# A gated delta rule inside a decoder kernel: its instructions emitted by one clock, in one order for all engines

## The chip, the cores and the metric

One NeuronCore of a Trainium2 chip runs the whole program. The metric is device microseconds (us) for one launch. The engines are named as in the profile: PE (matrix products and transposes; its weight loads are PEld), DVE (vector), ACT (activations, and one of the queues that issue DMAs), POOL (GpSimd) and SP (DMA issue only).

## What is computed

The program is a decoder of several blocks over 512 tokens of width 1024, in fp32. The change lies in one stage, the first half of `parallel_mixers`, after the first feed-forward block:

```python
proj = h @ w_in
qkv, z, a, bt, glu, gates = jnp.split(proj, offs, axis=-1)
qkv = jax.nn.silu(causal_depthwise_conv(qkv, gdn_conv_qkv))      # 4 taps
g = -jnp.exp(gdn_a_log) * jax.nn.softplus(a + gdn_dt_bias)
o = chunk_gated_delta_rule(q, k, v, g, jax.nn.sigmoid(bt))       # 8 heads of 128
o = rms_norm(o, gdn_norm_g) * jax.nn.silu(z)
c = c_lin * jax.nn.sigmoid(c_gate)                               # from glu
c = causal_depthwise_conv(c, conv_dw_w) + conv_dw_b              # 31 taps, 1024 channels
...
S_t = exp(g_t) S_{t-1} (I - beta_t k_t k_t^T) + beta_t k_t v_t^T ; o_t = S_t^T q_t
```

Each head is done in four chunks of 128 tokens. Within a chunk a triangular system is solved (a matrix Y, built from 16 by 16 blocks that are joined to 32, 64 and 128), and the state S passes from chunk to chunk.

## The kernel before

**Products.** A projection unit is one 128-column piece of `w_in`: `wload` (L326 to L332) brings 512 KB into `wr` (two buffers) by one DMA, ACT rounds it to `wh` (L323), and POOL makes the rest `wl` (L324, `now["lo"] = G` in this stage; DVE does it elsewhere). `wh` and `wl` have four buffers each. PE then makes 24 products of 128 by 512 (`mm3`, L212 to L214). The stage has 3 such units per head for q, k and v (`gdn_rows`), one for z (`gdn_z`), two per group of 128 channels of the long convolution (`glu_conv`), and eight gate units (`gate_proj`).

**Rows.** The end of a `gdn_rows` unit takes four taps (one on ACT, three on DVE, L818), Silu on ACT, four transposes on PE, and for k and q the inverse norm: squares on ACT (L770), a power on POOL.

**Decay and blocks.** `gdn_decay` makes exp of the cumulated gate (a broadcast by DMA from `gcrow`, an add on POOL, four exponentials on ACT, L843) and the matrices `mt` and `at`. `mt` goes to DRAM (`sm`). `gdn_blocks`, for a pair of heads, loads the 16 by 16 blocks (`ub`), inverts all 64 in 15 columns of two small DVE operations (L875, L877), writes them (`sy`, `sx`) and loads them back as Y and X.

**Heads.** `gdn_head` first joins the blocks to Y in eight steps, each of a few small products or transposes and one eviction (L918 to L938), then does 4 chunks of 3 dependent steps (PE, then ACT or DVE, then PE again), then the output: squares, small DVE operations, a power and a product on POOL (L982), four transposes (L218) and one DVE operation (L991).

**The long convolution.** 30 taps per group of 128 channels on DVE (L640, 240 in all), accumulating in one PSUM bank (`cv`).

**The order.** Two heads run as a chain, and `phase` interleaves it with filler (the projection units) by a credit of `pe_ns` per step. Work that follows a projection is put off by `after(8000.0, ...)`. `in_order(True)` ties PE to the order of emission. The order of the other engines is set by the scheduler's priorities: the long convolution stands 300 priorities later (`CONV_LATER`, L636), the block columns 100 (`BLOCKS_LATER`, L870). The weight DMAs are issued from ACT (`now["dq"] = A`), the small DMAs of the delta rule from SP.

After the stage come the other gate units, `split_o`, `gated(..., "w_gdn_out")` and `conv_norm`, whose transposes (L653) read all eight groups of the long convolution.

Of the kernel before, what the change touches and what calls it, by code (L numbers as in the profile page):

```python
# [26 lines left out]
CONV_LATER = 300  # L27
BLOCKS_LATER = 100
# [82 lines left out]
def kernel(ctx: ExitStack, tc: tile.TileContext, a: dict, out: bass.AP, upto=99):  # L111
    nc = tc.nc
    V, A, G, PE, S = nc.vector, nc.scalar, nc.gpsimd, nc.tensor, nc.sync
    n_names = [0]
# [77 lines left out]
    pe_ns = [0.0]  # L192
    order = {"on": False, "last": None}

    def placed(inst):

        if order["on"]:
            if order["last"] is not None:
                tc.add_manual_dep(inst.ins, order["last"].name, mybir.DependencyInfo(
                    mybir.DependencyClass.NoSync, mybir.DependencyReason.DATA), reason="order of emission")  # L200
            order["last"] = inst.ins

    def in_order(on):
        order.update(on=on, last=None)

    def mm(o, lhsT, rhs, start=True, stop=True):
        pe_ns[0] += 230.0
        placed(PE.matmul(o, lhsT, rhs, start=start, stop=stop))  # L208

    def mm3(o, lh, rh, start, stop):  # L210
        pe_ns[0] += 680.0
        placed(PE.matmul(o, lh[1], rh[0], start=start, stop=False))  # L212
        placed(PE.matmul(o, lh[0], rh[1], start=False, stop=False))  # L213
        placed(PE.matmul(o, lh[0], rh[0], start=False, stop=stop))  # L214

    def turn(o, x, i):
        pe_ns[0] += 110.0
        placed(PE.transpose(o, x, i))  # L218
# [25 lines left out]
    later = []  # L244

    def after(ns, work_):
        later.append((pe_ns[0] + ns, work_))

    def due(all_=False):

        for i, (t, work_) in enumerate(later):
            if all_ or t <= pe_ns[0]:
                del later[i]
                work_()
                return True
        return False

    def phase(chain, filler, share):

        filler, credit = iter(filler), 0.0  # L260

        def fill():
            before = pe_ns[0]
            if not due() and next(filler, None) is None:
                return None
            return pe_ns[0] - before + 20.0

        for _ in chain:
            credit += share
            while credit > 0:  # L270
                took = fill()
                if took is None:
                    break
                credit -= took
        while fill() is not None:
            pass
# [337 lines left out]
    def glu_conv(c0, c1):  # L614
        w = dram_w("w_in")
        act = acts["b1_1"]
        for c in range(c0, c1):
            if c % 2 == 0:
                cv.setdefault("out", []).append(slot(FT, tag="ma"))
            ps = []  # L620
            for base in (4112, 4112 + 1024):
                p = bank()
                h, l = wload(w, 0, 8, base + c * 128, 128)
                for k in range(8):
                    mm3(p, (h[:, k], l[:, k]), (act.hi(k), act.lo(k)), k == 0, k == 7)
                    if k % 2:
                        yield 1
                ps.append(p)
            pad = work("pad", (128, T + 30))
            V.memset(pad[:, :30], 0.0)  # L630
            A.copy(pad[:, 30:], ps[0])
            sg = work("xr", (128, T))
            A.activation(sg, ps[1], AF.Sigmoid)
            G.tensor_tensor(pad[:, 30:], pad[:, 30:], sg, OP.mult)
            o = cv["out"][c // 2][:, c % 2]
            with tc.high_priority(-CONV_LATER):  # L636
                s_ = bank(tag="cv")
                A.activation(s_, pad[:, 0:T], AF.Identity, bias=cols["convb"][:, c:c + 1], scale=tap31(0, c))  # L638
                for j in range(1, 31):
                    V.scalar_tensor_tensor(s_ if j < 30 else o, pad[:, j:j + T], tap31(j, c), s_, OP.mult, OP.add)  # L640
            yield 1
# [105 lines left out]
    def gdn_rows(h):  # L747
# [4 lines left out]
        kq = slot(FT, (128, 4, 2, 128), "ma")  # L752
        vk = slot(FT, (128, 2, 4, 128), "vk")
        v, kdec = vk[:, 0], vk[:, 1]
        left = [3]

        def ready():
            left[0] -= 1
            if not left[0]:
                gd["rows", h] = kq, v, kdec  # L760
# [11 lines left out]
        def of_v(x):  # L772
            A.copy(v, four_turned(x))
            ready()

        def of_q(x):
            r = tiny((128, 4))
            squares(r, four_turned(x))
            rq = gd["rq"][:, :, h]
            V.tensor_scalar(rq, r, 128.0, 128.0 * RMS_EPS, OP.mult, OP.add)  # L780
            G.tensor_tensor(rq, rq, nhalf[:, :4], OP.pow)
            ready()

        def of_k(x):
            p = four_turned(x)
            s_ = work("sq", (128, 4, 128))
            A.copy(s_, p)
            r = tiny((128, 4))
            squares(r, s_)
            inv_sqrt(r, r, 1.0, RMS_EPS, 4)  # L790
            G.tensor_tensor(s_, s_, r[:, :, None].to_broadcast([128, 4, 128]), OP.mult)

            def back():
                A.copy(kq[:, :, 0], four_turned(s_))
                G.tensor_tensor(kdec, s_, four(gd["kd"], h), OP.mult)
                ready()

            after(8000.0, back)

        for i, then in ((1, of_k), (0, of_q), (2, of_v)):  # L800
            if ("pre", h) in gd:
                p = gd["pre", h][i]
            else:
                hw, lw = wload(w, 0, 8, i * 1024 + h * 128, 128)
                p = bank()
                for k in range(8):
                    mm3(p, (hw[:, k], lw[:, k]), (act.hi(k), act.lo(k)), k == 0, k == 7)
                    if k % 2:
                        yield 1
# [15 lines left out]
            after(8000.0, lambda then=then, xf=xf: then(xf))  # L825
            yield 1
# [7 lines left out]
    def gdn_decay(h):  # L834
        while ("rows", h) not in gd:
            yield 1
        kq, v, kdec = gd["rows", h]
        dt_ = t2((128, 4, 128))
        src = gd["rows"][0:1, 0:1]
        S.dma_start(dt_, bass.AP(tensor=src.tensor, offset=src.offset + h * 128, ap=[[0, 128], [1024, 4], [1, 128]]))  # L840
        G.tensor_tensor(dt_, dt_, gneg[:, None, :].to_broadcast([128, 4, 128]), OP.add)
        for c in range(4):
            A.activation(dt_[:, c], dt_[:, c], AF.Exp, bias=gd["ngc"][:, c, h:h + 1], scale=1.0)  # L843
        yield 1
        yield 1
        mt, at = work("mt", (128, 4, 128)), work("at", (128, 4, 128))
        for cc in range(2):
# [9 lines left out]
            yield 1  # L857
        S.dma_start(chunks(gd["sm"], h % 2), mt)
        gd["decay", h] = [mt, at]
        yield 1  # L860

    def gdn_blocks(h):
# [6 lines left out]
        S.dma_start(ub, blocks(gd["sm"]))  # L869
        with tc.high_priority(-BLOCKS_LATER):  # L870
            V.memset(yb, 0.0)
# [1195 lines left out]
```

## Time and profile before

| | us |
|---|---|
| three runs | 2838.24 (median), 2834.88 to 2845.14 |
| profiled execution | 2842.67 |
| its span, first to last instruction | 2840.9 |
| PE busy | 2678.6 (94% of the span) |
| DVE, ACT, POOL busy | 1368.0, 1062.1, 473.1 |

The profiled execution lies 4.4 us over the median of the runs. Times are counted from the start of the span. A PE record's length is modelled and overlaps the next one, so for the pace of PE the distance from start to start is what to read. "Idle before" a row is what its engine waited, and behind the arrow stands what ended that wait. "issue" is a wait that the profile can't put down to anything.

### The profile page before, as it was taken

The page shows a single profiled execution, that of the slowest core. Times are in us where ns is not written, and L with a number is a line of the kernel's source. Part 1 is how long each engine was busy: PE and PEld are TensorE (multiplying, and loading weights), DVE is VectorE, ACT ScalarE, POOL GpSimd, SP SyncE. Part 2 cuts the span into 40 slices and gives each one's busy share as a digit, 9 for nine tenths or more (in the row PEclk, how much of TensorE's full clock was granted, in tenths as well). Part 3 has the DMA queues.
Part 4 walks back from the last instruction along what each step waited for, and adds up shares of the span by engine and source line. Part 5 has one row for each costly group of instructions (what it writes and reads, how often), then busy time and mean ns, then how long its engine had stood idle before and what let it go on. Part 6 is the DMA issues. An engine that isn't in the chain of part 4 may idle for free.

```text
span 2840.9 us, 34780 instructions
## 1 busy us (share of the span) xinstructions
PE 2678.6 (94%) x13600; PEld 2180.7 (77%) x13600; DVE 1368.0 (48%) x2476; ACT 1062.1 (37%) x1993; POOL 473.1 (17%) x341
## 2 busy tenths in 40 slices
PE   9999986788788999999999999999999999999998
PEld 7888875676666887988888876786687777888887
DVE  3232355665675356445222255476454464632324
ACT  4222235354333342342222244454255464232231
POOL 0101034333332012002100121031002000211010
PEclk9999998899899999999999999999999999999999
DMA  5223353554542523434323233322235122432332
GB/s 190 97 97 96 97 113 61 87 73 72 69 78 45 111 90 126 141 126 156 97 97 97 97 104 113 98 75 79 76 103 100 51 64 89 142 125 97 97 97 82
DMA packets 326324, 277.30 MB, mean 98 GB/s; under 512 B 50360, under 2 KB 278416, under 8 KB 326160
## 3 DMA queue, kind: packets, MB, share of 16 engines
q1 hardware_dynamic: 267072, 232.61, 27.8%
q10 hardware_dynamic: 59088, 42.47, 9.0%
q8 instruction: 107, 1.75, 0.3%
q14 instruction: 57, 0.47, 0.1%
HBM read 256.64 MB, written 20.49 MB: 98 GB/s over the span
## 4 chain that ended last, share of the span: by engine, by line
PE 46%; DVE 4%; POOL 1%; issue 1%; DMA 1%; ACT 1%; DVEq 0%; ACTq 0%; POOLq 0%; SPq 0%
PE mm L212 13%; PE mm L213 13%; PE mm L214 13%; PE mm L208 6%; DMA wr<-in_w_in 1%; DVE m L359 1%; DVE wl L324 1%; PE mm L1690 0%; POOL hr L348 0%; POOL t L1050 0%; ACT wh L323 0%; DVE m L358 0%; PE mm L1448 0%; PE mm L1740 0%; DVE mf L359 0%
## 5 line engine op out<-in xcount | busy, mean ns | idle before, releaser
L324 DVE TENSOR_TENSOR wl<-wr,wh 128x1024 fp32r<-128x1024 f32 (+1 forms) x351 | 427.4, 1218 | 826.5 <-ACT wh L323 825.2
L212 PE MATMUL mm<-x,wl 128*128 128x512 f32 (+3 forms) x2072 | 806.8, 389 | 2.7 <-DVE gsmall L703 2.5
L213 PE MATMUL mm<-x,wh 128*128 128x512 f32 (+3 forms) x2072 | 794.3, 383 | 0.0
L214 PE MATMUL mm<-x,wh 128*128 128x512 f32 (+3 forms) x2072 | 792.2, 382 | 0.0
L323 ACT CAST wh<-wr 128x1024 fp32r<-128x1024 f32 (+2 forms) x425 | 436.4, 1028 | 787.0 <-PE mm L214 529.1
L212 PEld LDWEIGHTS mm<-x,wl 128*128 128x128 f32 (+2 forms) x2072 | 395.9, 191 | 77.5 <-issue 6.6
L214 PEld LDWEIGHTS mm<-x,wh 128*128 128x128 f32 (+2 forms) x2072 | 395.2, 191 | 75.7 <-issue 1.4
L213 PEld LDWEIGHTS mm<-x,wh 128*128 128x128 f32 (+2 forms) x2072 | 396.3, 191 | 70.5 <-issue 1.2
L324 POOL TENSOR_TENSOR wl<-wr,wh 128x1024 fp32r<-128x1024 f32 x74 | 176.7, 2390 | 485.4 <-ACT wh L323 436.8
L324 POOL TENSOR_TENSOR h<-t,h 128x512 fp32r<-128x512 f32 x66 | 101.7, 1542 | 835.8 <-ACT h L323 835.8
L214 PE MATMUL mm<-wh,h 128*128 128x512 f32 x528 | 205.6, 389 | 0.0
L212 PE MATMUL mm<-wh,h 128*128 128x512 f32 x528 | 205.5, 389 | 0.0
L213 PE MATMUL mm<-wl,h 128*128 128x512 f32 x528 | 205.5, 389 | 0.0
L640 DVE SCALAR_TENSOR_TENSOR mm<-pad,cols,mm 128x512 f32<-128x512 f32 x232 | 174.5, 752 | 40.9 <-ACT mm L638 36.2
L214 PEld LDWEIGHTS mm<-wh,h 128*128 128x128 f32 x528 | 99.1, 188 | 20.6
L213 PEld LDWEIGHTS mm<-wl,h 128*128 128x128 f32 x528 | 99.1, 188 | 20.5
L212 PEld LDWEIGHTS mm<-wh,h 128*128 128x128 f32 x528 | 99.1, 188 | 20.4
L543 ACT ACTIVATE t<-mm 128x512 f32<-128x512 f32 x66 | 39.5, 599 | 127.8 <-PE mm L214 127.8
L544 DVE SCALAR_TENSOR_TENSOR t<-t,mm 128x512 f32<-128x512 f32 x66 | 45.4, 688 | 77.4 <-POOL h L324 54.9
L212 PE MATMUL mm<-m,wl 128*128 128x512 f32 (+1 forms) x224 | 81.7, 365 | 0.1
L214 PE MATMUL mm<-m,wh 128*128 128x512 f32 (+1 forms) x224 | 81.1, 362 | 0.0
L213 PE MATMUL mm<-m,wh 128*128 128x512 f32 (+1 forms) x224 | 80.9, 361 | 0.0
(454 smaller groups left out, 3684.8 us busy)
## 6 DMA issues: line engine op xcount, KB each, us to landing
wr<-in_w_in SPq DMA_DIRECT2D x69, 512.0 KB
wr<-in_w_in ACTq DMA_DIRECT2D x53, 512.0 KB
wr<-in_ffn_wg SPq DMA_DIRECT2D x44, 512.0 KB
wr<-in_ffn_wu SPq DMA_DIRECT2D x44, 512.0 KB
wr<-in_ffn_wd SPq DMA_DIRECT2D x44, 512.0 KB
wr<-in_w_ffn_in SPq DMA_DIRECT2D x44, 512.0 KB
wr<-in_w_ffn_out SPq DMA_DIRECT2D x22, 512.0 KB
xd<-m ACTq DMA_DIRECT2D x32, 256.0 KB
```

What stands on the lines that cost most here:

```text
L208: placed(PE.matmul(o, lhsT, rhs, start=start, stop=stop))
L212: placed(PE.matmul(o, lh[1], rh[0], start=start, stop=False))
L213: placed(PE.matmul(o, lh[0], rh[1], start=False, stop=False))
L214: placed(PE.matmul(o, lh[0], rh[0], start=False, stop=stop))
L323: A.copy(hi, src)
L324: (eng or V).tensor_sub(lo, src, hi.bitcast(FT))
L359: V.scalar_tensor_tensor(yh, yh, r, bh, OP.mult, OP.add)
L543: A.activation(sg, ps[0][f], AF.Silu)
L544: V.scalar_tensor_tensor(sg, sg, scale, ps[1][f], OP.mult, OP.mult)
L640: V.scalar_tensor_tensor(s_ if j < 30 else o, pad[:, j:j + T], tap31(j, c), s_, OP.mult, OP.add)
```

## The change

All emission in the stage goes through one loop. Every chain is a generator that yields nanoseconds of PE work (`yield 1300.0`), put in a list by `spawn`. The clock is `pe_ns`, which each product or transpose advances. `step` runs the chain that is due first, or else the next piece of a projection unit. `unit` may have a condition (`may`), and up to three units' weights are loaded ahead. Each engine but SP is then tied to the order of emission (`keep_order`). A second clock, `dve_ns`, adds 180 ns and 1.1 ns per element for each DVE instruction. `fill_dve` emits one item of background work, a block column or a tap of the long convolution, only where `dve_ns` is behind `pe_ns`. What is left of the taps when all else has been emitted is emitted then, and is not tied. The joins of a pair (`gdn_join`) are split off from `gdn_head`, and `gdn_pair` starts the decay of the next pair before them. The weight DMAs move to SP, the small DMAs to ACT. Two memsets move from DVE to POOL. The gate units move into the loop, as units that open when heads are done. The convolution's input is kept in its output tile and copied to `pad` when its taps begin. The products, and the taps, are the same in number.

```diff
+    def keep_order(start):
+        for inst in nc.cur_bb.bb.instructions[start:]:
+            if inst.engine == mybir.EngineType.SP:
+                continue
+            if inst.engine in last:
+                tc.add_manual_dep(inst, last[inst.engine].name, mybir.DependencyInfo(
                     mybir.DependencyClass.NoSync, mybir.DependencyReason.DATA), reason="order of emission")
...
+            if inst.engine == mybir.EngineType.DVE:
+                n = math.prod(k for _, k in inst.outs[0].ap[1:])
+                dve_ns[0] = max(dve_ns[0], pe_ns[0]) + 180.0 + 1.1 * n
...
+    def fill_dve():
+        while dve_ns[0] < pe_ns[0]:
+            todo = background[0] or background[1]
+            if not todo:
+                break
+            start = len(nc.cur_bb.bb.instructions)
+            todo.pop(0)()
+            keep_order(start)
...
-        S.dma_start(blocks(gd["sy"]), yb)
+        background[0].extend([lambda k=k: column(k) for k in range(15, 0, -1)])
+        yield from until(lambda: not background[0])
+        yield 1000.0
+        A.dma_start(blocks(gd["sy"]), yb)
         A.copy(ub, yb.rearrange("p a b -> p b a"))
-        S.dma_start(blocks(gd["sx"]), ub)
+        yield 1000.0
+        A.dma_start(blocks(gd["sx"]), ub)
+        yield 3500.0
         for t, s_ in (("Y", "sy"), ("X", "sx")):
             for i in range(2):
                 m = work(t, (128, 4, 128))
-                S.dma_start(m, chunks(gd[s_], i))
+                A.dma_start(m, chunks(gd[s_], i))
                 gd["decay", h + i].append(m)
-        yield 1
...
+        yield 4000.0
+    def gdn_pair(h):
+        spawn(gdn_decay(h))
+        spawn(gdn_decay(h + 1), 700.0)
+        yield from until(lambda: ("decay", h) in gd and ("decay", h + 1) in gd)
         yield from gdn_blocks(h)
...
+        if h < 6:
+            spawn(gdn_pair(h + 2))
+        spawn(gdn_join(h))
+        spawn(gdn_join(h + 1), 700.0)
...
-            run(gdn_start(), gdn_gates(), gdn_rows(0))
-            while due(True):
-                pass
+            run(gdn_start(), gdn_gates())
             banks(pj=3, tp=1, gt=3, cv=1)
...
+            while True:
+                fill_dve()
+                start = len(nc.cur_bb.bb.instructions)
+                if not step():
+                    break
+                keep_order(start)
+            for left in background[1]:
+                left()
```

**First place: PE at the gates.** Before, behind the last product of the gate projection (`mm_2795`) and the four transposes of its result (L694) stand the products of the first units; between them and L208, which needs the softplus that DVE makes of those transposes, stand 44 rows, 43 of them such products.

```order
L214 MATMUL mm_2795<-x_2456,wh_2790 16x512
L694 MATMUL mm_2822<-ident,xr_2820 128x16 x4
L212 MATMUL mm_2943<-x_2444,wl_2946 128x512
L213 MATMUL mm_2943<-x_2445,wh_2945 128x512
L214 MATMUL mm_2943<-x_2444,wh_2945 128x512
```

Now, on the same engine (L734 is L694 before; `gsmall` holds the gates):

```order
L214 MATMUL mm_2795<-x_2456,wh_2790 16x512
L734 MATMUL mm_2822<-ident,xr_2820 128x16 x4
L208 MATMUL mm_2858<-gsmall_2827,xr_2606 128x32 x2
L765 MATMUL mm_2862<-ident,gsmall_2827 32x128
L212 MATMUL mm_2911<-x_2444,wl_2895 128x512
L213 MATMUL mm_2911<-x_2445,wh_2894 128x512
```

L208 and L765 moved to stand directly behind the transposes, and the first unit behind them.

**Second place: DVE at the outputs of a pair of heads.** Before, for heads 4 and 5 (L991 reads the transposed output; `mm_5935` is the accumulator of one group of the long convolution):

```order
L925 TENSOR_TENSOR X_5907<-mm_6219,sqc_2607 128x512
L640 SCALAR_TENSOR_TENSOR mm_5935<-pad_5929,cols_300,mm_5935 128x512 x12
L640 SCALAR_TENSOR_TENSOR ma_5745<-pad_5929,cols_300,mm_5935 128x512
L991 SCALAR_TENSOR_TENSOR ma_6181<-mm_6176,cols_286,t_6018 128x512
L991 SCALAR_TENSOR_TENSOR ma_6181<-mm_6198,cols_286,t_6083 128x512
L925 TENSOR_TENSOR X_5909<-mm_6225,sqc_2607 128x512
```

Now, for heads 0 and 1 (L1052 is L991 before, L654 is L640; L902 and L904 are the next pair's decay):

```order
L654 SCALAR_TENSOR_TENSOR mm_4569<-pad_4566,cols_293,mm_4569 128x512
L843 TENSOR_SCALAR gsmall_2827<-tiny_4665 128x4
L654 SCALAR_TENSOR_TENSOR mm_4569<-pad_4566,cols_293,mm_4569 128x512 x3
L1052 SCALAR_TENSOR_TENSOR ma_4705<-mm_4724,cols_286,ma_4705 128x512
L654 SCALAR_TENSOR_TENSOR mm_4569<-pad_4566,cols_293,mm_4569 128x512 x4
L1052 SCALAR_TENSOR_TENSOR ma_4705<-mm_4772,cols_286,ma_4705 128x512
L902 SCALAR_TENSOR_TENSOR mt_4778<-mm_4780,gsmall_2827,t_4313 128x128 x2
```

Thirteen taps in one run ahead of an output became runs of three and four.

**Third place: DVE and PE at the end of the stage.** Before, DVE has no tap left behind the last outputs; L324 is the splitting of the heads' outputs (`m`) and of the next weights (`wl`):

```order
L991 SCALAR_TENSOR_TENSOR ma_6685<-mm_6680,cols_286,t_6502 128x512
L991 SCALAR_TENSOR_TENSOR ma_6685<-mm_6702,cols_286,t_6567 128x512
L324 TENSOR_TENSOR m_7121<-ma_4647,m_7120 128x512 x2
L324 TENSOR_TENSOR m_7127<-ma_5500,m_7126 128x512 x2
L324 TENSOR_TENSOR m_7133<-ma_6181,m_7132 128x512
L324 TENSOR_TENSOR wl_6864<-wr_6862,wh_6863 128x1024
```

Now, on DVE:

```order
L1052 SCALAR_TENSOR_TENSOR ma_6545<-mm_6618,cols_286,ma_6545 128x512
L654 SCALAR_TENSOR_TENSOR mm_6416<-pad_6413,cols_300,mm_6416 128x512
L1052 SCALAR_TENSOR_TENSOR ma_6545<-mm_6631,cols_286,ma_6545 128x512
L654 SCALAR_TENSOR_TENSOR mm_6416<-pad_6413,cols_300,mm_6416 128x512 x13
L347 TENSOR_TENSOR wl_6864<-wr_6862,wh_6863 128x1024
```

Behind the last L1052 now stand 75 taps (15 of group 5, and all 30 of groups 6 and 7), with the eight weight splits of the following projection (L347, which is L324 before) between them. On PE before, `conv_norm`'s transposes (L653; `ma_5745` holds groups 6 and 7) come behind the first product unit of `w_gdn_out` (`mm_7144`):

```order
L213 MATMUL mm_7144<-m_7139,wh_7146 128x512
L214 MATMUL mm_7144<-m_7138,wh_7146 128x512
L653 MATMUL mm_7178<-ident,ma_2942 128x128 x2
L653 MATMUL mm_7178<-ident,ma_3688 128x128 x2
L653 MATMUL mm_7185<-ident,ma_5206 128x128 x2
L653 MATMUL mm_7185<-ident,ma_5745 128x128 x2
```

Now, on PE (L693 is L653 before; `ma_5888` holds groups 6 and 7):

```order
L214 MATMUL mm_6990<-x_2456,wh_7023 128x512
L693 MATMUL mm_7178<-ident,ma_3023 128x128 x2
L693 MATMUL mm_7178<-ident,ma_3983 128x128 x2
L693 MATMUL mm_7185<-ident,ma_4959 128x128 x2
L693 MATMUL mm_7185<-ident,ma_5888 128x128 x2
L693 MATMUL mm_7200<-ident,ma_3023 128x128
L212 MATMUL mm_6991<-x_2444,wl_6994 128x512
```

They moved ahead of the last three of that projection's eight units (`mm_6991` is one of them) and of the first unit of `w_gdn_out`.

## Rows read from the trace of the kernel before

**Rows 1.** The page: busy time of PE; granted clock in 40 slices of the span.
```profile
PE 2678.6 (94%) x13600; PEld 2180.7 (77%) x13600; DVE 1368.0 (48%) x2476; ACT 1062.1 (37%) x1993; POOL 473.1 (17%) x341
...
PEclk9999998899899999999999999999999999999999
```

**Rows 2.** Windows: stretch, its length, busy PE, PEld, DVE, ACT, POOL; clock, DMA.
```profile
424.00:992.00 568.00, 463.33 (x2516) 381.47 (x2517) 335.62 (x645) 241.31 (x571) 181.66 (x112) 0.90 0.49 75
```

**Rows 3.** Waits of PE from 424 to 992 us: total, times, longest.
```profile
PE mm L218 <- POOL t L982: 23.8, 8, 8.7
PE mm L218 <- ACT ma L821: 20.3, 1, 20.3
PE mm L208 <- issue: 19.3, 2, 11.6
PE mm L208 <- DVE t L948: 9.9, 3, 3.8
PE mm L218 <- ACT t L770: 8.0, 2, 5.8
PE mm L208 <- DMA X<-sx: 7.7, 1, 7.7
PE mm L208 <- DVE at L856: 6.0, 2, 5.3
```

**Rows 4.** Timeline of PE, products spaced at high and at low clock.
```profile
570.40 0.39 PE L213 MATMUL mm<-x,wh 128*128 128x512 f32 x1
570.63 0.39 PE L214 MATMUL mm<-x,wh 128*128 128x512 f32 x1
...
868.48 0.63 PE L213 MATMUL mm<-x,wh 128*128 128x512 f32 x1
868.91 0.63 PE L214 MATMUL mm<-x,wh 128*128 128x512 f32 x1
```

**Rows 5.** Timeline of PE around the gates.
```profile
408.13 0.60 PE L694 MATMUL mm<-ident,xr 16*128 16x16 f32 x4 [2.39 <-ACT xr L691]
...
411.19 0.76 PE L212 MATMUL mm<-x,wl 128*128 128x512 f32 x1 [2.46 <-DVE gsmall L703]
...
424.16 0.63 PE L208 MATMUL mm<-gsmall,xr 128*128 128x32 f32 x4 [0.79 <-DVE gsmall L719]
```

**Rows 6.** Timeline of PE at the outputs of heads 2 and 3.
```profile
747.82 0.60 PE L208 MATMUL mm<-t,at 128*128 128x128 f32 x4
...
757.67 1.12 PE L218 MATMUL mm<-ident,t 128*128 128x128 f32 x4 [7.87 <-POOL t L982]
...
760.10 1.11 PE L218 MATMUL mm<-ident,t 128*128 128x128 f32 x4 [1.31 <-POOL t L982]
```

**Rows 7.** Timeline at the outputs of heads 4 and 5: DVE and PE.
```profile
855.21 9.46 DVE L640 SCALAR_TENSOR_TENSOR mm<-pad,cols,mm 128x512 f32<-128x512 f32 x12
...
866.21 2.05 PE L208 MATMUL mm<-X,mt 128*128 128x128 f32 x8 [11.65 <-issue]
```

**Rows 8.** Groups on DVE from 424 to 992 us: busy, mean ns, idle before.
```profile
L324 DVE TENSOR_TENSOR wl<-wr,wh 128x1024 fp32r<-128x1024 f32 x12 | 14.7, 1224 | 41.2 <-ACT wh L323 41.2
```

**Rows 9.** Timeline of the first pair's blocks: SP and PE.
```profile
541.34 0.60 SPq L878 DMA_DIRECT2D sy<-yb  x1
...
547.80 2.92 SPq L884 DMA_DIRECT2D X<-sx  x2
...
556.57 3.78 PE L208 MATMUL mm<-X,mt 128*128 128x128 f32 x16 [7.68 <-DMA X<-sx]
```

**Rows 10.** Groups on ACT from 424 to 992 us.
```profile
L956 ACT ACTIVATE t<-mm,gsmall 128x128 f32<-128x128 f32 x32 | 10.3, 366 | 11.6 <-POOL wl L324 9.8 <-PE mm L208 1.6
L843 ACT ACTIVATE t<-t,gsmall 128x128 f32<-128x128 f32 x32 | 10.2, 391 | 19.9 <-POOL t L841 19.9
```

**Rows 11.** Timeline of ACT: a table load and its neighbours.
```profile
742.04 0.81 ACT L949 ACTIVATE t<-mm,gsmall 128x128 f32<-128x128 f32 x2 [3.24 <-DVE t L948]
742.87 1.28 ACT L1005 ACT_TABLE_LOAD   x1
744.17 0.60 ACT L1005 ACTIVATE t<-mm 128x512 f32<-128x512 f32 x1
```

More of the change, by code (lines that the diff above doesn't have):

```diff
@@ L241, in interleave @@
             yield
[L244 to L255, printed above, removed]
-        return False
[L258 to L275, printed above, removed]
-            pass
+    procs, units, loaded, behind, background = [], [], [], [], [[], []]
@@ new lines, in spawn, with split_ahead @@
+    def spawn(g, ns=0.0):
+        procs.append([pe_ns[0] + ns, g])
+    def split_ahead(n):
+        for u in ([u for u in units if u["may"]()] + units)[:n]:
+            if u["w"] is None and sum(e["w"] is not None for e in units) < 3:
+                u["w"] = wload(*u["src"])
+    def fill_dve():
[6 more added lines that the diff above has]
+            keep_order(start)
@@ new lines, in step @@
+    def step():
+        due = [p for p in procs if p[0] <= pe_ns[0]]
+        if due:
+            p = min(due, key=lambda e: e[0])
+            ns = next(p[1], None)
+            if ns is None:
+                procs.remove(p)
+            else:
+                p[0] = pe_ns[0] + ns
+            return True
+        if not behind:
+            u = next((u for u in units if u["may"]()), None)
+            if u is not None:
+                units.remove(u)
+                if u["w"] is None:
+                    u["w"] = wload(*u["src"])
+                behind.append(u["body"](*u["w"]))
+                split_ahead(2)
+        if behind:
+            if next(behind[0], None) is None:
+                behind.pop()
+            return True
+        if procs:
+            pe_ns[0] = min(p[0] for p in procs)
+            return True
+        return False
@@ L279, with unit, until @@
+    def unit(src, body, may=lambda: True):
+        units.append({"src": src, "body": body, "may": may, "w": None})
+    def until(flag):
+        while not flag():
+            yield 500.0
     ident = cpool.tile([128, 128], FT, name="ident")
@@ L612, with glu_conv, taps, first @@
     cv = {}
-    def glu_conv(c0, c1):
+    def glu_conv(c):
         w = dram_w("w_in")
         act = acts["b1_1"]
-        for c in range(c0, c1):
+        ps = []
+        def taps(o):
+            s_ = []
+            def first():
+                pad = work("pad", (128, T + 30))
+                G.memset(pad[:, :30], 0.0)
+                A.copy(pad[:, 30:], o)
+                s_.extend((pad, bank(tag="cv")))
+                A.activation(s_[1], pad[:, 0:T], AF.Identity, bias=cols["convb"][:, c:c + 1], scale=tap31(0, c))
+            def tap(j):
+                pad, p = s_
+                V.scalar_tensor_tensor(p if j < 30 else o, pad[:, j:j + T], tap31(j, c), p, OP.mult, OP.add)
+            background[1].append(first)
+            background[1].extend([lambda j=j: tap(j) for j in range(1, 31)])
+        def consume():
@@ L630, in glu_conv @@
-            V.memset(pad[:, :30], 0.0)
-            A.copy(pad[:, 30:], ps[0])
+            o = cv["out"][c // 2][:, c % 2]
+            A.copy(o, ps[0])
             sg = work("xr", (128, T))
             A.activation(sg, ps[1], AF.Sigmoid)
[L634 to L640, printed above, removed]
@@ L641, in glu_conv, with body @@
-            yield 1
+            yield 1500.0
+            G.tensor_tensor(o, o, sg, OP.mult)
+            yield 1500.0
+            taps(o)
+        def body(h, l):
+            p = bank()
+            for k in range(8):
+                mm3(p, (h[:, k], l[:, k]), (act.hi(k), act.lo(k)), k == 0, k == 7)
+                yield 1
+            ps.append(p)
+            if len(ps) == 2:
+                spawn(consume())
+        unit((w, 0, 8, 4112 + c * 128, 128), body)
+        unit((w, 0, 8, 4112 + 1024 + c * 128, 128), body, lambda: bool(ps))
@@ L751, in gdn_rows, with made @@
         act = acts["b1_1"]
[L752 to L755, printed above, removed]
+        tiles, left = [], [3]
+        def made():
+            if not tiles:
+                kq = slot(FT, (128, 4, 2, 128), "ma")
+                vk = slot(FT, (128, 2, 4, 128), "vk")
+                tiles.extend((kq, vk[:, 0], vk[:, 1]))
+            return tiles
         def ready():
@@ L770, in squares, with post @@
                 A.activation(t1(), x[:, c], AF.Square, accum_out=r[:, c:c + 1])
[L772 to L809, printed above, removed]
+        def post(i, p):
+            kq, v, kdec = made()
             x = work("xr", (128, T))
@@ L938, in gdn_head @@
                     A.mul(Y[q, :, r], p[q, :, r], -1.0)
-            yield 1
+            yield JOIN_NS
+        gd["joined", h] = True
+    def gdn_head(h):
+        kq, v, kdec = gd["rows", h]
+        mt, at, Y, X = gd["decay", h]
         o = t2((128, 4, 128))
@@ L943, in gdn_head @@
             r = t1()
+            if c == 2:
+                gd["late", h] = True
             if c:
```

211 lines of the change are left out of this document (114 added, 97 removed).

## The prediction, made before the changed kernel ran

> **What bounds the kernel now.** I read the page first: PE is busy 2678.6 us, 94% of the span, and in the clock line the seventh, eighth and eleventh of 40 slices of 71 us (426 to 568, 710 to 781 us) stand a tenth below the others [rows 1]. So PE sets the time, and most of the program has little to give. The stage that the change rewrites is the exception. From 424 us, where the gates are ready, to 992 us, 568 us later, PE is busy 463.3 us: **104.7 us idle**, at a mean clock of 0.90, while DVE, ACT and POOL are busy 336, 241 and 182 us [rows 2]. No engine is full, so it is order and latency that cost here, which is what the change addresses.
>
> The waits of PE say what ends the idle time [rows 3]. The seven groups make 95.0 of the 104.7 us, and the reader is to see that no single one carries it: the outputs' POOL product (23.8 us in 8 waits), the first Silu chain (20.3 in one), two waits without a named releaser (19.3), the states (9.9), the norms (8.0), the first X (7.7) and the decay (6.0). All are places where PE reached a dependent step before another engine had done its part, although other products were still to be made.
>
> The idle time has a second price. Products stand 0.23 us apart at full clock (2.4 GHz) and 0.43 us at the low one (1.2 GHz) [rows 4]. A mean of 0.90 between levels 0.5 and 1 is a fifth of 568 us at the low level, 114 us. Of that the six long idles listed (20.3, 11.6, 8.7, 7.7, 5.8, 5.3) fill 59 us, and I put one more of the POOL waits at 8 us. About 47 us is left in which PE worked at half speed; half of that, **23 us**, was lost. It can be no more than 27 us, with the eighth idle at nothing. Together 127.7 us lie open.
>
> **The change, part by part.** *Gates.* The transposes of the gates start at 408.13 us and L208 at 424.16 us; between them PE makes the first unit's products from 411.19 us on [rows 5]. Those 43 products (the order's count) at 0.23 us cover 9.9 us of a chain on DVE that the change leaves alone. L208 now stands directly behind the transposes, so PE waits some 15 us there, and the products must be made later: **+9.9 us**.
>
> *Outputs.* The last state product of heads 2 and 3 starts at 747.82 us, and the output transposes 9.85 us later, at 757.67 us, the second ones at 760.10 us: squares, a power and the POOL product lie between, and PE idles 7.87 us of it [rows 6]. For heads 4 and 5 the cause is other: a run of 12 taps holds DVE for 9.46 us, and PE stands 11.65 us [rows 7]. Runs of three or four taps take 2.4 to 3.2 us, so the second kind should vanish, and the first be covered by units, except in the last pairs, where few units are left: the schedule sets some 7 us of PE work over a chain of 9.9 to 12.3 us. I charge 5 us for two pairs (0 to 12).
>
> *Tail.* Of 240 taps 75 are emitted behind the last output, and the transposes of `conv_norm`, which read the last of them, stand ahead of three projection units. Seen from the last output, DVE needs 75 taps at 0.788 us (9.46/12, [rows 7]), 59.1 us, eight weight splits at 1.224 us [rows 8], 10 us, one output operation of 0.75, two ACT starts of a group at some 1.5 us (two 0.6 us operations and their handing over) and some 4.5 us in which a split waits for a buffer that PE still reads: 77.5 us. PE has 228 products ahead of L693, 52.4 us at 0.23, and a us of transposes. PE waits 77.5 − 53.4, about **24, say 25 us**. Bounds: 17 with no split waiting and the group starts hidden, 32 if splits and taps alternate badly. Nothing behind it covers it, since L693 is ahead of those units in PE's order; moved taps are thus no saving, only moved.
>
> *Blocks and DMAs.* The reading back of X is issued at 547.80 us and PE starts at 556.57 us, 8.8 us later, 7.68 us of it idle [rows 9]. The plan gives 4 us of PE work between that issue and the joins. The issues now stand on ACT, in order behind its other work, and no longer on SP; SP gets the large weight DMAs, three units ahead. I charge 4 us for each of four pairs, **16 us** (0, if the joins start late anyway, to 5 each). On ACT an issue that waits for a landing holds all that is behind it: the exponentials of the decay wait for the broadcast of the cumulated gate, and with them the next evictions. **5 us** at the start (0 to 15).
>
> *Joins.* Eight dependent steps per pair, of two heads interleaved with units at 1.3 us. ACT's queue holds the next pair's four exponentials at 0.39 us [rows 10], and a table load of 1.28 us [rows 11]; ahead of a join's eviction 0 to 7 us per pair. I take the middle, 3.5 us, **14 us** in all. Chunk steps on the same queue: 1.5 us per pair, **6 us** (0 to 20). The units' own Silu and norms are put off by a clock instead of a fixed 8 us: **4 us** (0 to 12). The low clock after the waits that remain (gates, tail, perhaps two of the X): before, 23 us fell to seven idles, 3.3 us each, so **13 us** (7 to 20).
>
> In rows 11 the load ends at 744.15 us and the next activation starts at 744.17 us, and the operation before it had ended 0.02 us ahead: the switch costs 1.28 us here. The Trainium skill, page "ScalarE: Activation LUTs", section "What ACT_TABLE_LOAD costs", adds a drain of about 1380 ns to the load, some 2.66 us per switch; this trace shows none. By that rule, two loads per pair of heads would cost an estimated 11 us more, and the sum would be about 2819 us.
>
> *Sum.* 127.7 − 9.9 − 25 − (5 + 16 + 14 + 6 + 5 + 4 + 13 = 63) = 30 us gained. The profiled execution took 2842.7 us, 4.4 us over the median of the runs: 2842.7 − 30 = 2812.7, and against the median **2808 us**. Products, transposes, taps and weight bytes are the same in number and cost nothing new. The copy to `pad` (eight of 0.6 us on ACT) and two memsets on POOL lie on engines busy under half of the stage; without that cover they would be 6 us.
>
> **The rivals.**
> *R1, the order is nearly perfect.* The schedule leaves small gaps at most: the new waits are 15 to 30 us in place of 63, and 2842.7 − 93 + 25 gives about 2775 profiled, 2770 us. For it: the other engines have more than 230 us free each [rows 2], and three units are loaded ahead. Against it: nothing in the schedule knows how long ACT and POOL are busy; its delays are fixed numbers shorter than the chains seen (4 for 8.8 us, 7 for 9.9 us).
>
> *R2, new waits take the place of the old.* If each pair waits 5 us for X, 12 us in its joins (1.5 us in each of eight steps) and 6 us in chunks and outputs, four pairs give 92 us, and the time is 2838 us as before. For it: the order of ACT and POOL is now tied too, so one late instruction holds others that were ready, where before the scheduler let them pass. Against it: most of these steps have a unit's products between them.
>
> *R3, slower: ACT's one queue.* Each pair has 20 steps (8 joins, 12 in the chunks) in which an ACT eviction may stand behind an unrelated activation, a table load or a DMA issue that waits; 80 pair-steps. The start and X waits (21 us) stay. With 93 us to give, the kernel becomes slower by over 14 us once a step is held 86/80, some 1.08 us. A table load of 1.28 us in front of each [rows 11] would do it: 102 + 21 − 93 = 30 us slower, 2868 us. Against it: the evictions of the chunks take 0.37 us [rows 10], ACT is busy 241 of 568 us, and the instruction order lists 23 table loads in the stage against 26 before, far from 80.
>
> *R4, the DVE clock doesn't do what it says.* It reckons 743 ns for a tap (180 + 1.1 × 512) where the trace has 788. Were DVE behind at the last output by five to ten taps more, PE's wait in the tail would be 29 to 33 us: 2812 to 2816. This lies inside the forecast.
>
> **How the numbers follow.** About 0.5%, 14.2 us, is what a measurement of this kernel can tell from no change. The forecast with its bounds (gain of 14 to 70 us) has 0.60, R4 in it; R1 beyond that 0.12; R2, within 14 us either way, 0.19; R3 0.09. So faster 0.72, same 0.19, slower 0.09. For 8 in 10 the range takes the forecast and the nearer part of R2: new waits of 23 us give 2768, of 93 us 2838. Range **2768 to 2838 us**. R1's far part and R3 are left out.
>
> **What would show it.** In the profile of the changed kernel: PE stands 13 to 15 us before L208 at the gates, and at the end 17 to 32 us before L693, ended by a DVE tap, with 75 taps behind the last output. The POOL waits at the outputs and the wait behind twelve taps are gone or under 2 us each; each pair has a wait of 0 to 5 us on X. In the stage between, PE's idle time is 50 us or so, and ACT ends most of it, in the joins. The forecast is wrong if the tail's wait is absent, if joins and chunks together hold PE for more than 60 us (R2, R3), or if the middle shows under 20 us of idle (R1).

## The result, and the profile after

The changed kernel is **slower by 1.7%**: 2888.38 us (median of four runs, 2885.95 to 2888.98) against 2838.86, ratio 1.0171 with a 95% interval of 1.0151 to 1.0190. The forecast was 2808 us, in a range that ended at 2838. The experiments below ran on several chips, each beside the kernel before; so they are compared by their ratios to it, and 0.0010 of ratio is 2.84 us.

The page of the changed kernel's profiled execution (2888.98 us), as [rows 1] for before: busy time of PE and the granted clock in 40 slices.

```profile
span 2887.2 us, 34809 instructions
...
PE 2704.2 (94%) x13600; PEld 2193.2 (76%) x13600; DVE 1368.0 (47%) x2460; ACT 1066.4 (37%) x1999; POOL 477.7 (17%) x357
...
PEclk9999989889899799999999999999999999999999
```

The span grew by 46.3 us, from 2840.9. PE is busy 25.6 us longer with the same 13600 instructions, so a little over half of the loss is PE at work at a lower clock; the other 20.7 us are idle time. The windows show where (columns as in [rows 2]; the last row is the kernel before in the second stretch):

```profile
424.00:992.00 568.00, 473.72 (x2471) 385.20 (x2471) 311.06 (x595) 245.19 (x574) 195.83 (x133) 0.88 0.51 73
992.00:1100.00 108.00, 91.13 (x419) 74.54 (x420) 65.65 (x87) 36.57 (x51) 6.07 (x7) 0.91 0.28 86
...
992.00:1100.00 108.00, 107.50 (x502) 88.15 (x501) 60.20 (x70) 39.13 (x52) 12.57 (x12) 1.00 0.35 111
```

In the stage, PE idles 94.3 us where it idled 104.7, at a clock of 0.88 instead of 0.90: the new order gains next to nothing. In the next 108 us it idles 16.9 us at 0.91; before, the same stretch had 0.5 us and a clock of 1.00. Lined up by the number of PE instructions done, the changed kernel is 1.6 us late where the kernel before stands at 400 us, and 38 us late where it stands at 1000 us. The waits of PE from 400 to 1120 us, to be held against [rows 3]:

```profile
PE mm L212 <- POOL wl L347: 37.1, 10, 5.8
PE mm L693 <- DVE ma L654: 29.2, 2, 24.1
PE mm L208 <- DMA X<-sx: 10.1, 2, 5.1
PE mm L208 <- issue: 9.8, 1, 9.8
PE mm L218 <- ACT t L814: 9.0, 6, 2.4
PE mm L218 <- ACT Y L992: 6.2, 2, 3.6
PE mm L208 <- ACT t L1017: 5.2, 2, 4.2
PE mm L208 <- ACT X L982: 4.6, 3, 2.8
PE mm L218 <- POOL sq L852: 4.4, 2, 4.0
PE mm L218 <- ACT xr L833: 2.8, 2, 2.6
```

The largest of the old waits are gone: none at the outputs (23.8 us before), none behind a run of twelve taps, none of 20 us on a first Silu. Those for the norms (L814, 8.0 us before) and for X (7.7 us) are still there. The first line is new, and no line of before answers to it: ten times PE comes to a projection unit whose weights POOL has not yet split. The second is the tail, as forecast: 75 taps behind the last output.

PE at the gates, as [rows 5]: two waits where 43 products had stood.

```profile
407.94 0.41 PE L734 MATMUL mm<-ident,xr 16*128 16x16 f32 x4 [0.67 <-ACT xr L731]
418.18 1.03 PE L208 MATMUL mm<-gsmall,xr 128*128 128x32 f32 x4 [9.82 <-issue]
...
425.70 0.79 PE L212 MATMUL mm<-x,wl 128*128 128x512 f32 x1 [5.81 <-POOL wl L347]
```

Why the products aren't there, SP's and ACT's timelines tell:

```profile
378.89 6.39 SPq L353 DMA_DIRECT2D wr<-in_w_in  x3
```

```profile
419.25 0.69 ACT L824 ACTIVATE xr<-mm,cols 128x512 f32<-128x512 f32 x1 [7.15 <-PE mm L208]
...
421.71 0.38 ACTq L885 DMA_DIRECT2D t<-gcrow  x1
422.18 1.99 ACT L346 CAST wh<-wr 128x1024 fp32r<-128x1024 f32 x2 [1.92 <-DMA gcrow<-t]
```

The weights of the first units were asked for by 385 us. ACT rounds them (L346) only at 422 us: in its tied order they stand behind a tap that waits 7 us for PE, and behind a small DMA that needs the gates' result. So ACT waited for PE's L208, which waited for DVE's gates, and then PE waited for ACT's rounding and POOL's split.

A late unit in mid-stage, on ACT, POOL and PE:

```profile
825.80 0.58 ACT L663 COPY ma<-mm 128x512 f32<-128x512 f32 x1
826.39 1.28 ACT L665 ACT_TABLE_LOAD   x1
827.68 0.60 ACT L665 ACTIVATE xr<-mm 128x512 f32<-128x512 f32 x1
828.18 1.98 ACT L346 CAST wh<-wr 128x1024 fp32r<-128x1024 f32 x2
```

```profile
829.29 4.67 POOL L347 TENSOR_TENSOR wl<-wr,wh 128x1024 fp32r<-128x1024 f32 x2 [8.26 <-ACT wh L346]
```

```profile
825.56 0.39 PE L208 MATMUL mm<-t,at 128*128 128x128 f32 x2
831.69 0.80 PE L212 MATMUL mm<-x,wl 128*128 128x512 f32 x1 [5.74 <-POOL wl L347]
832.28 0.63 PE L213 MATMUL mm<-x,wh 128*128 128x512 f32 x1
832.71 0.63 PE L214 MATMUL mm<-x,wh 128*128 128x512 f32 x1
```

Rounding starts over 2 us after PE ran dry, the split follows it, and PE then works at 0.43 us a product, the low pace of [rows 4]. So this wait is paid twice, as idle time and as slow products behind it. Among ACT's own waits from 400 to 1120 us the largest group, twelve times and 50 us in all, is a rounding whose DMA has not landed.

```profile
ACT wh L346 <- DMA wr<-in_w_in: 50.4, 12, 8.9
```

The tail, on PE, and one row of DVE from it:

```profile
983.81 0.47 PE L693 MATMUL mm<-ident,ma 128*128 128x128 f32 x1 [5.04 <-DVE ma L654]
1008.42 0.69 PE L693 MATMUL mm<-ident,ma 128*128 128x128 f32 x2 [24.14 <-DVE ma L654]
```

```profile
944.22 1.23 DVE L347 TENSOR_TENSOR wl<-wr,wh 128x1024 fp32r<-128x1024 f32 x1 [10.70 <-ACT wh L346]
```

Between the last output (922.60 us) and the last tap (1008.37 us) DVE stands some 16 us for ACT's roundings, 10.7 of them in this row.

### The profile page after: what moved, and what is told of

Its sections match the earlier page's. It is cut to its first block, busy times and chain, and to the rows that moved or that the text cites. A ratio compares the mean times of both kernels' runs of the same rounds, so it can differ in the third digit from the quotient of the medians.

```text
span 2887.2 us, 34809 instructions
## 1 busy us (share of the span) xinstructions
PE 2704.2 (94%) x13600; PEld 2193.2 (76%) x13600; DVE 1368.0 (47%) x2460; ACT 1066.4 (37%) x1999; POOL 477.7 (17%) x357
## 5 line engine op out<-in xcount | busy, mean ns | idle before, releaser
L212 PE MATMUL mm<-x,wl 128*128 128x512 f32 (+3 forms) x2072 | 813.5, 393 | 41.2 <-POOL wl L347 37.1
L347 DVE TENSOR_TENSOR wl<-wr,wh 128x1024 fp32r<-128x1024 f32 (+1 forms) x351 | 428.4, 1221 | 794.3 <-ACT wh L346 793.1
L346 ACT CAST wh<-wr 128x1024 fp32r<-128x1024 f32 (+2 forms) x425 | 436.3, 1027 | 804.4 <-PE mm L214 488.6
L347 POOL TENSOR_TENSOR wl<-wr,wh 128x1024 fp32r<-128x1024 f32 x74 | 176.7, 2392 | 577.1 <-ACT wh L346 562.8
L347 POOL TENSOR_TENSOR h<-t,h 128x512 fp32r<-128x512 f32 x66 | 101.7, 1541 | 838.6 <-ACT h L346 838.6
L654 DVE SCALAR_TENSOR_TENSOR mm<-pad,cols,mm 128x512 f32<-128x512 f32 x232 | 174.7, 753 | 22.6 <-ACT mm L650 17.0
L214 PEld LDWEIGHTS mm<-wh,h 128*128 128x128 f32 x528 | 99.1, 188 | 20.6
L826 DVE SCALAR_TENSOR_TENSOR xr<-mm,cols,xr 128x511 f32<-128x511 f32 (+2 forms) x72 | 53.8, 748 | 65.6 <-ACT xr L824 64.0
L214 PE MATMUL mm<-m,wh 128*128 128x512 f32 (+1 forms) x224 | 81.3, 363 | 0.0
```

The costliest lines, as they stand in the source:

```text
L346: A.copy(hi, src)
L347: (eng or V).tensor_sub(lo, src, hi.bitcast(FT))
L654: V.scalar_tensor_tensor(p if j < 30 else o, pad[:, j:j + T], tap31(j, c), p, OP.mult, OP.add)
```

## The experiments

Three things in the emission were under suspicion. The second unit of a long-convolution group opens only when the first is done, so the loading ahead passes it over, and it is asked for when it starts. The DVE clock is set to PE's and then 743 ns past it at each tap, so a step of 680 ns lets no second tap through. And ACT and POOL are tied to the order of emission.

**First four runs: one suspicion each.** a1 drops the second unit's condition, a2 lets the DVE clock stay behind, a3 does both, a4 takes ACT and POOL out of the tie.

```diff
-        unit((w, 0, 8, 4112 + 1024 + c * 128, 128), body, lambda: bool(ps))
+        unit((w, 0, 8, 4112 + 1024 + c * 128, 128), body)
```

```diff
-                dve_ns[0] = max(dve_ns[0], pe_ns[0]) + 180.0 + 1.1 * n
+                dve_ns[0] = max(dve_ns[0], pe_ns[0] - 2000.0) + 180.0 + 1.1 * n
```

```diff
-            if inst.engine == mybir.EngineType.SP:
+            if inst.engine in (mybir.EngineType.SP, mybir.EngineType.Activation, mybir.EngineType.Pool):
                 continue
```

> The condition on the second unit of a long-convolution group (it opens only when the first is done) is dropped, so that its weights are loaded ahead like the others'. Theory L (late loads): 37 us of PE's idle time, ended by the POOL split, comes from units whose weights are asked for only when the unit starts; they are these second units. L expects that wait to fall from 37.1 us in 10 to under 12 us in 3 or 4, and with some 5 us of low clock a time near 2857 us. Theory Q (queues): the splits are late because ACT and POOL are tied to one order and do other work first. Q expects the wait to stay above 28 us and 2880 to 2890 us.

Ratio 1.0084 (1.0067 to 1.0101), 2867.98 us. The wait on the split fell to 13.8 us in 3, of which 5.8 is the one at the gates; L had said under 12. The time fell by 25 us in ratio (0.0087), 11 us less than L's 2857. L is right that these units were asked for too late; half of the loss stays. The waits of a1:

```profile
PE mm L693 <- DVE ma L654: 29.5, 2, 24.1
PE mm L208 <- DMA X<-sx: 15.7, 3, 6.2
PE mm L212 <- POOL wl L347: 13.8, 3, 5.8
```

> The DVE clock may stay up to 2 us behind PE's instead of being set to it, so that unused time isn't lost and the taps run at DVE's capacity. Theory T (taps): 75 taps are left over because each tap sets the clock 743 ns past PE's, and a step of 680 ns then lets none through. T expects no tap behind the last output, the wait before L693 gone (29.2 us, with 3 us of low clock behind it) and 2855 to 2860 us. Its rival D: taps set closer together on DVE, in a tied order, stand before the chains' small operations and cost there what the tail gives back: 2875 to 2890 us, with PE's waits on DVE lines up by 15 us or more.

1.0155 (1.0139 to 1.0170), 2886.24 us: 4.5 us in ratio, and the interval overlaps that of the change, so no gain is shown, though no tap is left behind and PE's wait for one has vanished. In its place the wait on the split grew from 37.1 to 42.6 us and that on X from 10.1 to 18.5. The time is where D put it; the wait isn't, as no DVE line is over 2.8 us.

> The edits of the two runs before together. L and T are at different places and add up: 2823 to 2830 us, below the kernel before the change. Q with D: 2870 to 2890 us.

1.0073 (1.0058 to 1.0088), 2864.0 us. Against a1 the tail's 29.5 us are gone, and the gain of 3 us lies within the intervals. The time is in neither expectation, nearer to Q with D. The waits of a3 (424 to 1100 us) show where the rest went: against a1 the splits (13.8 us there), the norms (9.4) and Silu (2.8) wait longer, X (15.7) hardly, and no DVE line comes near 15 us. So what D says of the sum holds, that the tail's gain is lost again in the middle, but not through waits for DVE.

```profile
PE mm L212 <- POOL wl L347: 20.8, 5, 5.8
PE mm L208 <- DMA X<-sx: 16.1, 2, 10.6
PE mm L218 <- ACT t L814: 13.2, 8, 5.4
...
PE mm L218 <- ACT xr L833: 7.9, 7, 2.2
```

> The change, but ACT and POOL are not tied to the order of emission; the scheduler places their work by its priorities, PE and DVE stay tied. Theory Q (in-order queues of ACT and POOL hold the splits and evictions): the POOL wait falls under 15 us and ACT's waits (some 27 us) by half, 2845 to 2860 us. Theory L: the late splits are asked for no earlier, the POOL wait stays above 25 us, 2880 to 2895 us.

**0.9952** (0.9935 to 0.9968), 2830.39 us: faster than the kernel before, with nothing else touched. Of PE's order only the gates' L208 and L765 moved, behind 32 rows of the first units. Theory Q is right on the tie, and its time (2845 to 2860 us) was too careful: the wait on the split is 10.4 us in one, and the gates' waits of 9.8 and 5.8 us shrink to 3.0 and 2.6, since the first units' rounding no longer stands behind the gates. Its other sign failed: the waits that ACT ends don't halve but grow, from 31.6 to 40.1 us in all, with 18.7 for the norms (L814).

**Which part of the tie.** b1 unties ACT alone. b2 unties only the rounding and the split of the weights:

```diff
+        at = len(nc.cur_bb.bb.instructions)
         split(raw[:, :n], hi[:, :n], lo[:, :n], eng or now["lo"])
+        loose.update(i.name for i in nc.cur_bb.bb.instructions[at:])
...
-            if inst.engine == mybir.EngineType.SP:
+            if inst.engine == mybir.EngineType.SP or inst.name in loose:
```

> The change with ACT alone not tied; POOL, PE and DVE stay tied. Untying both gave 2830 us, 58 us under the change. Theory A (ACT's order is what costs): 2828 to 2838 us, PE's wait on the POOL split under 15 us. Theory P (POOL's order costs as much): the splits stay late, 2850 to 2880 us.

1.0029 (1.0017 to 1.0040), 2851.82 us: 40 us back in ratio, with 20.0 us on the split in 4 waits. That is at the edge of P's range: with ACT free, POOL's tie still costs some 22 us (0.9952 against 1.0029).

> The change with only the rounding of the weights on ACT and their split on POOL left out of the tied order; all other work of ACT and POOL is tied. Theory W (the weights' two operations stand too far back in the order, or hold it while their DMA is on its way): nearly all of the 58 us comes back, 2828 to 2840 us, the gates' waits of 9.8 and 5.8 us gone. Theory E (the evictions, Silu and squares of the chains are what is held): under 20 us comes back, 2868 to 2888 us, ACT's waits in the joins and norms as before.

**1.0004** (0.9994 to 1.0013), 2843.4 us: 47 us of the 62 us that a4 gives back in ratio (0.0167 of 0.0219) hang on the weights' two operations. Theory W holds, 3 us outside its range; the wait on the split is 2.9 us. The first units are now rounded from 395.57 us on, where the change begins at 422.18. Not every wait shrinks: Silu (L835, 2.8 us in the change) waits 14.1 us. ACT's first roundings in b2, PE's waits from 400 to 1100 us, and the page:

```profile
395.57 1.05 ACT L346 CAST wh<-wr 128x1024 fp32r<-128x1024 f32 x1 [5.57 <-PE mm L214]
398.45 1.05 ACT L346 CAST wh<-wr 128x1024 fp32r<-128x1024 f32 x1 [1.83 <-PE mm L214]
```

```profile
PE mm L695 <- DVE ma L656: 24.9, 2, 24.3
PE mm L208 <- DMA X<-sx: 14.4, 3, 5.2
PE mm L218 <- ACT xr L835: 14.1, 2, 11.5
...
PE mm L212 <- POOL wl L347: 2.9, 1, 2.9
```

```profile
PE 2687.2 (95%) x13600; PEld 2182.8 (77%) x13600; DVE 1378.4 (49%) x2460; ACT 1067.1 (38%) x1999; POOL 477.8 (17%) x357
```

Of the 50.2 us by which its span is shorter than the change's (2837.0), PE is busy 17 us less: part of the clock comes back with the waits.

**Too late, or in the way?** d1 keeps every tie, drops the second unit's condition and asks for weights three units ahead:

```diff
-                split_ahead(2)
+                split_ahead(3)
```

> The change with everything still tied, the second units' condition dropped (2868 us by itself) and weights asked for three units ahead instead of two (the weight buffers allow it). Theory P (place: in the tied order the rounding comes too late after its data): an earlier place helps, 2838 to 2856 us, and the gates' waits of 9.8 and 5.8 us stay. Theory B (blocking: a tied rounding holds ACT until its DMA lands, 50 us in 12 waits): asked for earlier, it holds ACT longer, those waits grow past 60 us, and the time is 2866 to 2880 us.

1.0114 (1.0097 to 1.0131), 2874.72 us: no better than a1. The time is in B's range, but the run doesn't show B. ACT's wait for the DMA grew to 58.6 us in 15 (53.7 in a1), just under the 60 of theory B; in b1, 40 us faster than the change, the same wait is 82.0 us in 21. All idle time of ACT in front of the roundings between 400 and 1000 us is 65.7 us in the change and 85.9 in b2, so b2 didn't gain by freeing ACT of it. Here the group in d1, then in b1:

```profile
ACT wh L346 <- DMA wr<-in_w_in: 58.6, 15, 10.0
...
ACT wh L346 <- DMA wr<-in_w_in: 82.0, 21, 15.1
```

Nor does d1 do away with theory P. The place at the gates didn't move in it: the first rounding starts at 422.38 us, and beside the gates a1 had only 8.0 us of waits for splits left to gain. So at the gates it is the place in the order that costs, as the change and b2 show; whether elsewhere a rounding costs more by coming late or by holding up what stands behind it, no run separates.

**The DMA queues.** c4 moves the six small DMA issues of decay and blocks from ACT to SP, in the change as it stands.

```diff
-        A.dma_start(ub, blocks(gd["sm"]))
+        S.dma_start(ub, blocks(gd["sm"]))
...
```

> The change with one edit: the small DMAs of the decay and the blocks go out from SP, as before the change, so that SP carries them behind the weights and ACT issues none. If ACT, holding its queue until a DMA's data is ready, is what makes the rounding late, 2860 to 2875 us and ACT's waits down by half. If the issues cost ACT little, 2884 to 2892 us, or up to 2900 us where a small DMA now stands behind a weight DMA that waits for its buffer (waits on X above the 10 us of the change).

1.0142 (1.0126 to 1.0159), 2882.51 us, 8 us less in ratio with intervals that just overlap, and 34.6 us on the split. Between the two expectations, nearer the second: the issues on ACT are at most a small part.

**Building on what helps.** b4 is a4 with a1's edit; b3 adds the credit.

> ACT and POOL untied and the second units' condition dropped. The one wait of 10.4 us on a late split goes, the tail's stays: 2816 to 2824 us. If the scheduler already moved the late weights ahead, 2826 to 2834 us.

**0.9903** (0.9878 to 0.9928), 2812.64 us, a little beyond the expectation; PE no longer waits for a split.

> ACT and POOL untied, the second units' condition dropped, and the DVE credit of 2 us, all three. If the tail's wait (20.8 us with ACT and POOL untied) is a loss by itself, 2798 to 2808 us. If what the tail gives comes back as waits for DVE in the middle, as it did in a3 (29 us gone, 4 us gained), 2815 to 2825 us.

0.9912 (0.9888 to 0.9935), 2817.76 us. The tail's wait is gone again and nothing is gained. c3 unties DVE too, to see whether its order is to blame:

```diff
-            if inst.engine in last:
+            if inst.engine == mybir.EngineType.PE and inst.engine in last:
```

> ACT, POOL and also DVE not tied (PE alone is), the second units' condition dropped, the credit of 2 us throughout. With DVE tied this took 2818 us, no better than without the credit. If it is DVE's tied order that puts taps ahead of the chains' operations, 2793 to 2803 us. If the scheduler puts them there as well, 2812 to 2825 us.

0.9929 (0.9907 to 0.9951), 2820.28 us: not DVE's tie. Early taps cost the middle the same when the scheduler places them. c1 and c2 put them later instead, where few chains are left:

```diff
-                dve_ns[0] = max(dve_ns[0], pe_ns[0]) + 180.0 + 1.1 * n
+                dve_ns[0] = max(dve_ns[0], pe_ns[0] - (2000.0 if ("late", 6) in gd else 0.0)) + 180.0 + 1.1 * n
```

> ACT and POOL untied, the second units' condition dropped, and the DVE credit of 2 us only from the middle of head 6 on, when few chain steps are left to stand behind taps: 37 taps instead of 58 behind the last output. If the tail is priced by the number of taps left (0.79 us each), 21 fewer take 16 of the 21 us wait, and with nothing given back in the middle it is 2796 to 2803 us. If taps cost the chain the same wherever they are put, 2810 to 2818 us as without it.

**0.9856** (0.9841 to 0.9871), 2801.9 us, the lowest of all, and as expected in number only: the tail still waits 15.3 us (21.0 in b4) and not 5. The stage is shorter for another reason, its clock of 0.95.

```profile
PE mm L693 <- DVE ma L654: 15.3, 1, 15.3
...
PE mm L208 <- DMA X<-sx: 2.3, 1, 2.3
```

```profile
424.00:992.00 568.00, 506.50 (x2782) 417.11 (x2783) 375.70 (x677) 267.81 (x609) 187.09 (x128) 0.95 0.52 82
```

Most of that clock isn't the edit's. In the traces of b4 and c1 the order of PE's products is the same throughout, and that of ACT, DVE and POOL is the same until 851 us of b4, where the first of c1's taps stands earlier. Yet c1 is already 19 us ahead there, with nearly the same waits (45.2 and 43.6 us over the products that b4 makes from 424 to 820 us). b4, then c1:

```profile
424.00:820.00 396.00, 350.28 (x1963) 287.08 (x1964) 243.05 (x484) 195.57 (x486) 166.24 (x112) 0.91 0.55 79
...
424.00:820.00 396.00, 351.69 (x2050) 289.44 (x2051) 249.49 (x494) 201.10 (x497) 168.79 (x113) 0.95 0.56 81
```

Behind that place c1 gains 6 us more, about what its tail waits less. By the medians it is 13 us faster than b4 in ratio (0.9856 against 0.9903, each on its own chip; b4's profiled run is its slowest of four, by 11 us). How much of this is the edit's stays open.

> As the run before, with the credit from the end of head 5 on: 13 taps are left, so the tail's wait is gone (21 us), but the chunk steps of heads 6 and 7 stand behind taps. 2793 to 2800 us if these steps have units beside them; 2805 us or more, and over 2802 for certain, if they wait for DVE.

0.9869 (0.9844 to 0.9894), 2808.23 us, not to be told from c1: the tail's wait is gone, and one state product waits 9.2 us for DVE.

> Only the weights' two operations untied (2843 us), with the second units' condition dropped and the DVE credit from the middle of head 6 on; all other work of ACT and POOL is tied. With ACT and POOL free altogether the same edits gave 2802 us. If the weights' operations are all that the tie harms, 2802 to 2810 us. If the tie harms the chains' other ACT work too (the 13 us between 2843 and 2830), 2812 to 2824 us.

0.9975 (0.9959 to 0.9991), 2835.8 us; c1, the same but for the tie, has 0.9856. This is above both expectations. The tie harms the chains' other work too: by 34 us against c1, by 15 us where a4 and b2 differ in the same way (0.9952 and 1.0004). In d2 PE waits 14.8 us on X (2.3 in c1) and 12.3 on a Silu. Its busy time is 2690.8 us against 2670.2 in c1, so 20.6 of the 35.8 us between their spans are clock, and with c1's clock above the 34 us may be too many.

## Why the prediction was wrong

**What was right.** The tail: 29.2 us against 25 (17 to 32), in the place forecast and ended by a tap. DVE's part of the reckoning was short, though: from the last output transposes to the last tap it took 86 us and not 77.5, as it stood some 16 us for ACT's roundings. X: 10.1 us, in two waits, against 16. Joins: 6.2 and 4.6 us on ACT's evictions against 14. Chunk steps: 5.2 and 2.3 us against 6. The outputs (5 charged) and the start (5): no wait.

**What came out by luck, or was too small.** At the gates L208 waited 9.8 us and not 13 to 15, since the way from the transposes to L208 took 10.2 us instead of 16. The 5.8 us that fill this up to some 15 are a wait for the first split, which the forecast didn't have. The units' own Silu and norms were charged 4 us and cost 17.6 (9.0, 4.4, 2.8 and two of 0.7). The named waits add up to some 85 us, where 90 were foreseen (15 + 25 + 16 + 14 + 6 + 5 + 5 + 4); the sum is that close because such errors cancel.

**The step that failed first** is a term that the sum lacks. The working charged the units nothing for their weights and put down, in R1, that "three units are loaded ahead". Three is the cap; the code asks for the first two units in line (`split_ahead(2)`), and the ones that open late are passed over: a1 shows some 25 us for that. Nor does loading ahead help where the rounding is tied: at the gates it stood, data at hand, behind work that waited for PE. The wait on the split measured 37.1 us in 10, and b2, which frees only the rounding and the split, takes back 47 us. None of PE's waits before has such a line; there the scheduler placed these operations, and POOL was busy 182 of 568 us [rows 2], so its share of time gave no warning. The working looked at ACT's tied queue for evictions and DMA issues, and not for the rounding.

**The second** is the clock. It was put as 23 us to win and 13 us to lose again. Instead PE's busy time rose by 25.6 us. From 400 to 1120 us PE waited 110 us in 33 waits before and 125 us in 44 now; which of the two, the sum or the number, costs the clock, no run separates. The split's 37 us and the 36 us between the forecast and the measured clock make about 73 of the 76 us from 2812.7, the profiled time forecast, to 2888.98.

The signs that the forecast named for its being wrong didn't show: the tail's wait is there, joins and chunks hold PE for some 18 us and not 60, and the middle idles far more than 20. What showed instead is a line that it didn't ask for.

**R3** named the right queue and the side on which it ended: ACT, in order. It put the delay on 80 evictions at 1.08 us and judged it unlikely since the evictions are short and table loads few. Most of the delay hangs on the 60 roundings of weights and their splits; b2 leaves the evictions tied and is back at the time before. That the chains' work suffers too, a4 against b2 and d2 against c1 show, but as X, Silu and clock. R2's sum (new waits eat the gain) describes the stage itself: 94.3 us idle against 104.7. R4 played no part: the taps ran late because the clock gives away unused time (a2 leaves none), not by its 743 against 788 ns.

The table load again takes 1.28 us with the next activation 0.01 us after it (826.39 to 827.68 us above). The Trainium skill, page "ScalarE: Activation LUTs", section "What ACT_TABLE_LOAD costs", would have 1.38 us more; this trace, like the one before, shows none.

**Open.** Lined up by PE instructions, from 1870 to 2340 us of the kernel before, the changed kernel loses some 8 us more, in code that the change doesn't touch, and the variants some 6, c1 too. The instruction order of PE there differs from before. Why the scheduler orders it otherwise, and whether that is the cause, wasn't tried.

## What to carry to other kernels

When an order is tied on an engine, read every kind of instruction on that engine, above all the one that prepares data for the engine that sets the time: here a rounding that b2 makes from 395 us on began at 422 us. Tie the engine that sets the time and leave the feeding ones to the scheduler, at least for the loads (1.0171 to 0.9952 here by untying two engines, 1.0004 by untying the loads' two operations). Work moved off the end is a gain only where the place that it moves to has room: 29 us of tail gave 3 to 5 us, no more than the intervals allow for, when the taps went ahead of the chains (a2, a3). That c1, which puts them where few chains are left, does better is not shown beyond some 6 us.

## What was not expected of the hardware

The granted clock is a cost beside idle time. The change and c1 run the same 13600 PE instructions in 2704.2 and 2670.2 us of busy time; those 34.0 us are over a third of the 91.2 us between their spans (2887.2 and 2796.0). And the clock isn't a property of the order alone: b4 and c1, with one order of products throughout and of ACT, DVE and POOL up to 851 us, were granted 0.91 and 0.95 from 424 to 820 us, and one stood 19 us ahead of the other by 851 us. A gain of that size between two single profiles is no proof of an edit.
